# Seven-product pairs in the V chunk and three more in the first attention chunk of a hybrid encoder layer

## The chip, the cores and the metric

One NeuronCore of a Trainium2 chip. The metric is the device time of one execution in microseconds (us), as the median of several runs. Beside the runs stands one profiled execution, from which all durations in this text come.

## The reference

One layer on 256 tokens of width 4096: a first layer norm, one input projection to 13,312 columns, two parallel branches, one output projection, the residual and a last layer norm. All inputs and outputs are float32.

```python
h = layer_norm(x, emb_ln_g, emb_ln_b)
p = h @ w_in                                  # 4096 -> 13312
y_conv = c_b * centred_short_conv(c_c * c_h, conv_w) * jax.nn.silu(c_z)
y_attn = banded_window_attention(a_q, a_k, a_v, sink) * jax.nn.silu(a_z)
y = jnp.concatenate([y_conv, y_attn], axis=-1) @ w_out
out = layer_norm(DN_ALPHA * h + y, ln_g, ln_b)
```

The four kv heads make K and V 512 columns wide each; the sixteen query heads are taken four at a time.

## The kernel before, in words

**Chunks and steps.** The columns of `w_in` are cut into 26 chunks of 512. The first is K, the second V; then come, for each of four head groups, the gate of the attention branch (`C_AZ`) and the queries (`C_Q`); then the convolution's chunks. `w_out` follows in nine chunks. A chunk's sum over the 4096 rows, 32 blocks of 128 ("k-tiles"), is made in steps, which one list (`IN_STEPS`) puts in order. This text numbers the steps from K's first, 0. K has the steps 0 to 7, V 8 to 15, the first attention chunk (the gate of head group 0) 16 to 25, the queries behind it begin with 26.

**Kinds of step.** Everything is multiplied as float32r with a split: a number is kept as a high part and a remainder (low part), and a product takes high by high, high by low and low by high.
- A *plain* step ("s") takes four k-tiles, for two halves of the tokens, two halves of the columns and three products: 48 matmuls of 256 columns (`mm`, line 251). The 32 with the weights' high part come first, then the 16 with the low part.
- A *pair* step ("S") takes two k-tiles as a 2 x 2 matrix of blocks and needs seven block products in place of eight: 7 x 3 = 21 matmuls (`mm_pair`, lines 276 and 277 with the high part, 14 matmuls, then 279 with the low part, 7). It needs sums of blocks of x (made once for each pair of k-tiles, `x_sums`, kept in `SC`) and of blocks of the weights (made for every step, `sums`, lines 183 to 185).
- A *half* step ("h") takes two k-tiles in the plain way: 24 matmuls.

`PAIRS` gives the number of pairs of each chunk and `ORDERS` the order of its steps: 0 pairs, `"ssssssss"`; 4 pairs (`NP1`), `"sssSSsSsSs"`; 7 pairs (`NP`), `"sSShSsSSsSSs"`. A chunk of p pairs takes its first 2p k-tiles by pairs.

**What each engine does in step j** (the loop at line 805): TensorE multiplies step j. ScalarE writes the high part of the weights of step j + 3 (`split_hi`, line 204), then what is due at that step (`later`). VectorE does what is due, then `x_sums` if the step is in `X_SUMS`, then the block sums of step j + 4 if that is a pair, then the low part of step j + 3 (`split_lo`, line 208). SyncE issues the loads of coming pieces as buffers come free. Every engine executes its list in the order in which it is written; there is no scheduler.

**Buffers.** There are three tiles for high parts (`whi`), three for low parts (`wlo0` to `wlo2`), three for loaded pieces (`w0` to `w2`), and a fourth (`w6`) from the end of the prologue on. A chunk's sums stand in two of four PSUM tiles (`acc`). A chunk with pairs uses two more PSUM banks (`pacc`), of which there are only two: the first pair of the next chunk opens them again, after `pair_sums` has read them. Before, the first chunk with pairs is the first attention chunk.

**Chunk ends.** A chunk without pairs is taken from PSUM at the end of its last step (`chunk_end`). For a chunk with pairs `pair_copy` and `pair_sums` (lines 679 to 682) turn the two banks into sums in SBUF right behind its last pair, and four steps behind the chunk's last step `whole` (line 687) adds what stands in `acc`. K is copied out, transposed and split (`k_turn`, one step later); V is split into high and low part straight from PSUM (`end_v`), for two of the heads into `v` and for the others into `vlate`, which goes to DRAM for later.

**x.** The prologue normalises x, turns it (`hT`) and splits it into `xT`, four k-tiles at a time (`x_split(q)`, lines 385 and 386). The first eight k-tiles of K are multiplied straight from `hT`, so that K doesn't need their split. `x_sums(p)` makes the sums of pair p (four on VectorE from `xs`, lines 645 and 650, then high parts on ScalarE and low parts on VectorE, `halves`, lines 497 and 498) and overwrites one block of `xT` with one of them; so it can stand only behind the last plain step that uses these two k-tiles.

Of the kernel before, what the change touches and what calls it, by code (L numbers as in the profile page):

```python
# [34 lines left out]
NPC = KT // PK  # L35
IN_ORDER = [C_K, C_V]
# [5 lines left out]
HT = S // 2  # L42
NP = 7
NP1 = 4
PAIRS = [0, 0, NP1] + [NP] * (len(IN_ORDER) - 3)
ORDERS = {0: "s" * 8, NP1: "sssSSsSsSs", NP: "sSShSsSSsSSs"}
OUT = 100
OP = 4
# [6 lines left out]
def units(ci):  # L55


    q, p, us = -(-2 * PAIRS[ci] // PK), 0, []
    for u in ORDERS[PAIRS[ci]]:
        if u == "s":  # L60
            us.append(("in", ci, q))
            q += 1
        elif u == "h":
            us.append(("half", ci, PAIRS[ci]))
        else:
            us.append(("pair", ci, p))
            p += 1
    assert q == NPC and p == PAIRS[ci]
    return us
# [18 lines left out]
def npairs(ci):  # L88
    return PAIRS[ci] if ci < OUT else OUT_ORDERS[ci - OUT].count("S")

# [10 lines left out]
def encoder_kernel(ctx: ExitStack, tc: tile.TileContext, x, emb_g, emb_b, wi, ws, conv_w, sink, wo, ln_g, ln_b, out):  # L101
# [28 lines left out]
    def w_bufs(j):  # L130

        bs = [(wpool, f"w{k}") for k in range(N_W)] + (extra if j < N_IN else [])
        if j >= N_IN and R is not None:
            late = j > in_R[0][0]
            bs += [(None, name) for last, name in in_R if j <= last and late == (name == "R2")]
        last_user = lambda b: max(u for c, u in user.items() if c == b or b[1] == "R2" and c[0] is None) if (
            b in user or b[1] == "R2") else -1
        return min((last_user(b), k) for k, b in enumerate(bs)), bs

    def load(j, to=None):  # L140
        kind, a, b = steps[j]
        if to is None:
            (_, k), bs = w_bufs(j)
            pool, name = bs[k]
            user[bs[k]] = j
            if pool is None:
                to = raw[j] = {"R0": R[:, 0, D // 2:D], "R1": R[:, 1, D // 2:D], "R2": R[:, :, 3 * D // 4:D]}[name]
            else:
                to = raw[j] = pool.tile([P, PIECE], F32, name=name, bufs=1)
        src = {"in": (wi, IN_PIECES), "out": (wo, OUT_PIECES)}.get(kind, (ws, ALL_PAIRS))  # L150
        src = src[0][src[1].index((a, b))]
        if len(to.shape) == 3:
            if is_pair(j):
                nc.sync.dma_start(out=to[:, 0, :], in_=src)
            else:
                nc.sync.dma_start(out=to, in_=src.rearrange("p (i n) -> p i n", i=2))
        else:
            nc.sync.dma_start(out=to[:, 0:src.shape[1]], in_=src)
# [43 lines left out]
    def split_hi(j):  # L202
        wh[j] = half_tile(j, "whi")
        nc.scalar.activation(part(j, wh[j]), part(j, raw[j]), AF.Copy)  # L204

    def split_lo(j):
        wl[j] = half_tile(j, "wlo")
        nc.vector.tensor_tensor(part(j, wl[j]), part(j, raw[j]), part(j, wh[j]).bitcast(F32), op=ALU.subtract)  # L208
        raw.pop(j)

    def split(j):
        if j < len(steps):
            split_hi(j)
            split_lo(j)
# [14 lines left out]
    for name in ("whi", "w0", "w1", "w2", "wlo0", "m", "nm", "wlo1", "den", "es", "wlo2"):  # L229
        n = {"whi": PIECE + GAP}.get(name, PIECE + 2 * OFF if name[:3] == "wlo" else PIECE if name[0] == "w" else 2)  # L230
# [3 lines left out]
    acc = {}  # L234
# [58 lines left out]
    with tc.tile_pool(name="pro", bufs=1) as pro:  # L293
# [62 lines left out]
        def transp2(q, tiles=(0, 1)):  # L356
            for half in range(2):
                if tiles[0] == 0:
                    pair[q, half] = ps_att.tile([P, 2, S], F32, name="att")
                for k in range(2):  # L360
                    kt = q * 4 + half * 2 + k
                    for i in tiles:
                        nc.tensor.transpose(pair[q, half][:, k, i * P:(i + 1) * P], xs[i][:, kt * P:(kt + 1) * P],  # L363
                                            ident)
# [18 lines left out]
        def x_split(q):  # L383
            sl = slice(q * 4, q * 4 + 4)
            nc.vector.tensor_copy(xT[:, sl, 0:S], hT[:, sl, :])
            nc.vector.tensor_tensor(xT[:, sl, S:2 * S], hT[:, sl, :], xT[:, sl, 0:S].bitcast(F32), op=ALU.subtract)
# [49 lines left out]
        turned2(5)  # L436
        x_split(5)
        split(5)
        load(8)
        transp2(6)  # L440
        mm(4)
        turned2(6)
        x_split(6)
        split(6)
        load(9)
        transp2(7)
        mm(5)
# [4 lines left out]
        mm(6)  # L452
        split(8)
        load(11)
        x_split(0)
        split(9)
        load(12)
        x_split(1)
    n_pro = 7


# [13 lines left out]
    def build_tab():  # L475
        ti = pa.tile([P, 2, S], F32, name="ti", tag="s")
        nc.gpsimd.iota(ti, pattern=[[-P, 2], [1, S]], base=0, channel_multiplier=-1,
                       allow_small_or_imprecise_dtypes=True)
        tf = pa.tile([P, 2, S], F32, name="tf", tag="p", bufs=2)
        nc.vector.tensor_scalar(tf, ti, -1.0, None, op0=ALU.mult)  # L480
        nc.vector.tensor_tensor(tf, tf, ti, op=ALU.max)
        nc.vector.tensor_scalar(ti, tf, float(WINDOW), NEG, op0=ALU.is_gt, op1=ALU.mult)
        nc.vector.tensor_tensor(tab, ti, tf, op=ALU.subtract)
# [12 lines left out]
    def halves(hi, lo, src):  # L496
        nc.scalar.activation(hi, src, AF.Copy)
        nc.vector.tensor_tensor(lo, src, hi.bitcast(F32), op=ALU.subtract)
# [18 lines left out]

    def end_v(ci, g):
        late = pa.tile([P, 2, 2, 2, P], F32R, name="vlate", tag="qhl")
        for i in range(2):  # L520
            ps = acc.pop((ci, i)).rearrange("p (a n) -> p a n", a=4)
            halves(v[:, :, i, 0, :], v[:, :, i, 1, :], ps[:, 0:2, :])
            halves(late[:, :, i, 0, :], late[:, :, i, 1, :], ps[:, 2:4, :])
        nc.sync.dma_start(out=vd, in_=late.bitcast(F32))
# [159 lines left out]
    def whole(ci):  # L684
        t = st_.pop(("e", ci))
        for i in range(2):
            nc.vector.tensor_tensor(t[:, i, :], acc.pop((ci, i)), t[:, i, :], op=ALU.add)
        return t
# [63 lines left out]
        for hi, lo, y in y_parts(q):  # L752
            nc.vector.tensor_tensor(lo, y, hi.bitcast(F32), op=ALU.subtract)

    X_SUMS = [NPC + 2 + k for k in range(NP1)] + [2 * NPC + k for k in (1, 4, 6)]
    build_tab()
    later = {}

    def at(j, fn, *a):
        later.setdefault(j, []).append((fn, a))  # L760

    ENDS = [(C_AZ, end_z), (C_V, end_v), (C_K, end_k), (C_Q, end_q), (C_CZ, end_cz), (C_CH, end_ch), (C_CC, end_cc),
            (C_CB, end_cb)]

# [32 lines left out]
    nxt = n_pro + 6  # L797
    last0 = N_IN - len(ORDERS[PAIRS[-1]])
    for t, f, q in ((3, y_load, 0), (5, y_hi, 0), (6, y_lo, 0), (6, y_load, 1), (7, y_hi, 1), (8, y_lo, 1), (8, y_load, 2),
# [5 lines left out]
    for j in range(n_pro, N_IN):  # L805
        kind, ci, q = steps[j]
# [8 lines left out]
        if kind == "pair" and q == PAIRS[ci] - 1:  # L815
            pair_copy(ci)
            at(j + 1, pair_sums, ci)
        if j in X_SUMS:
            x_sums(X_SUMS.index(j), pa.tile([P, 4 * S], F32, name="xs", tag="zT", bufs=2))
        if steps[j + 1][1] != ci or j == N_IN - 1:  # L820
# [235 lines left out]
    n = ncs - 1  # L1056
# [78 lines left out]
```

## Time and profile before

| | before |
|---|---|
| time, median of 3 runs (lowest to highest) | 1506.08 us (1505.47 to 1506.26) |
| the profiled execution, its time | 1505.99 us |
| the profiled execution, span of its instructions | 1504.3 us |
| TensorE's granted clock, mean | 0.999 |
| bytes moved by DMA | 316.18 MB, 210 GB/s on average |

The span runs from the first to the last instruction of the core; the execution's own time is 1.7 us longer. The profile was read by its list of engines, the chain of work that ended last, the table of who waited for whom, the timeline of each engine (start in us, length in us, engine, line, operation, output from input, count, and in brackets the idle time before it and what ended it) and busy times by stretches of time.

### The profile page before, as it was taken

The numbers are of one execution on the slowest core, as the hardware profiler recorded it, in microseconds if no ns is written. First come the engines' busy times: TensorE is split into PE (matmuls) and PEld (weight loads), VectorE is DVE, ScalarE is ACT, GpSimd is POOL, SyncE is SP. The second block draws the span as 40 slices with busy tenths as digits, with TensorE's granted clock in tenths as the row PEclk, the third lists the DMA queues.
The fourth block names the chain that finished last, engine by engine and source line by source line (L and its number), as shares of the span: only waits on it lengthen the run. The fifth ranks groups of instructions, "written<-read, shape, count | busy, mean of one in ns | idle before, by whom it ended". The sixth has DMA issues, their size and how long they took to land.

```text
span 1504.3 us, 30113 instructions
## 1 busy us (share of the span) xinstructions
PE 1490.8 (99%) x12947; PEld 1475.4 (98%) x12947; DVE 1329.7 (88%) x1555; ACT 781.7 (52%) x669; POOL 1.3 (0%) x7
## 2 busy tenths in 40 slices
PE   7999999999999999999999999999999999999998
PEld 4999999999999999999999999999999999999997
DVE  7768989999899998999899999999899688888876
ACT  4545556656566665545555455544556444444431
POOL 0000000000000000000000000000000000000000
PEclk9999999999999999999999999999999999999999
DMA  7555555656555555656556655656557656766673
GB/s 289 217 182 197 210 197 170 208 183 207 196 186 190 181 186 206 233 197 238 187 195 218 220 197 196 220 184 227 205 206 297 261 204 219 261 217 217 219 261 123
DMA packets 71749, 316.18 MB, mean 210 GB/s; under 512 B 8544, under 2 KB 12608, under 8 KB 50880
## 3 DMA queue, kind: packets, MB, share of 16 engines
q1 hardware_dynamic: 70608, 312.43, 58.7%
q8 instruction: 101, 1.65, 0.4%
q10 hardware_dynamic: 1008, 1.84, 0.3%
q14 instruction: 32, 0.26, 0.1%
HBM read 305.23 MB, written 8.91 MB: 209 GB/s over the span
## 4 chain that ended last, share of the span: by engine, by line
PE 98%; DVE 1%; DMA 0%; ACT 0%; SPq 0%; issue 0%; ACTq 0%
PE acc L251 45%; PE acc L923 20%; PE pacc L276 6%; PE pacc L277 6%; PE pacc L279 6%; PE acc L277 4%; PE acc L276 4%; PE acc L279 4%; PE att L493 1%; PE att L618 1%; DVE st L330 0%; PE att L604 0%; PE acc L380 0%; DMA x<-in_x 0%; PE att L363 0%; DVE x L338 0%
## 5 line engine op out<-in xcount | busy, mean ns | idle before, releaser
L204 ACT ACTIVATE whi<-w 128x2048 fp32r<-128x2048 f32 (+1 forms) x354 | 621.7, 1761 | 593.8 <-DVE w L185 231.0
L208 DVE TENSOR_TENSOR wlo<-w,whi 128x2048 fp32r<-128x2048 f32 (+1 forms) x354 | 736.1, 2083 | 102.7 <-ACT whi L204 83.6
L251 PE MATMUL acc<-whi,xT 128*128 128x256 f32 x3952 | 474.0, 276 | 0.0
L251 PEld LDWEIGHTS acc<-whi,xT 128*128 128x128 f32 x3952 | 459.9, 188 | 0.0
L251 PE MATMUL acc<-wlo,xT 128*128 128x256 f32 x1976 | 245.8, 275 | 0.0
L251 PEld LDWEIGHTS acc<-wlo,xT 128*128 128x128 f32 x1976 | 234.0, 188 | 0.0
L923 PE MATMUL acc<-whi,xT 128*128 128x256 f32 x1696 | 201.8, 275 | 0.0
L923 PEld LDWEIGHTS acc<-whi,xT 128*128 128x128 f32 x1696 | 196.6, 188 | 0.4 <-issue 0.4
L183 DVE TENSOR_TENSOR w<-w 128x512 f32<-128x512 f32 x179 | 122.4, 684 | 8.3 <-DMA w<-in_ws 8.3
L923 PE MATMUL acc<-wlo,xT 128*128 128x256 f32 x848 | 105.3, 275 | 0.0
L276 PE MATMUL acc<-whi,xT 128*128 128x256 f32 x370 | 102.1, 276 | 0.0
L277 PE MATMUL acc<-whi,xT 128*128 128x256 f32 x370 | 102.1, 276 | 0.0
L923 PEld LDWEIGHTS acc<-wlo,xT 128*128 128x128 f32 x848 | 100.4, 188 | 0.0
L276 PE MATMUL pacc<-whi,xT 128*128 128x256 f32 x350 | 98.2, 281 | 0.0
L277 PE MATMUL pacc<-whi,xT 128*128 128x256 f32 x350 | 96.5, 276 | 0.0
L279 PE MATMUL pacc<-wlo,xT 128*128 128x256 f32 x350 | 96.2, 275 | 0.0
L279 PE MATMUL acc<-wlo,xT 128*128 128x256 f32 x370 | 92.8, 275 | 0.0
L277 PE MATMUL pacc<-whi,SC 128*128 128x256 f32 x330 | 91.0, 276 | 0.0
L276 PE MATMUL pacc<-whi,SC 128*128 128x256 f32 x330 | 91.0, 276 | 0.0
L279 PE MATMUL pacc<-wlo,SC 128*128 128x256 f32 x330 | 82.9, 275 | 0.0
L184 DVE TENSOR_TENSOR w<-w 128x256 f32<-128x256 f32 x179 | 76.1, 425 | 6.2
L185 DVE TENSOR_TENSOR w<-w 128x256 f32<-128x256 f32 x179 | 76.1, 425 | 6.2
(220 smaller groups left out, 1674.3 us busy)
## 6 DMA issues: line engine op xcount, KB each, us to landing
w<-in_wi SPq DMA_DIRECT2D x112, 1024.0 KB
w<-in_ws SPq DMA_DIRECT2D x202, 512.0 KB
w<-in_wo SPq DMA_DIRECT2D x41, 1024.0 KB
R<-in_wo SPq DMA_DIRECT2D x13, 1024.0 KB
x<-in_x SPq DMA_DIRECT2D x7, 512.0 KB
yl<-yd SPq DMA_DIRECT2D x7, 512.0 KB
xc<-in_x SPq DMA_DIRECT2D x14, 256.0 KB
R<-in_ws SPq DMA_DIRECT2D x6, 512.0 KB
```

The costliest lines, as they stand in the source:

```text
L183: nc.vector.tensor_tensor(s01, b22, b12.to_broadcast([P, 2, HW]), op=ALU.add)
L184: nc.vector.tensor_tensor(r(6), r(5), r(1), op=ALU.add)
L185: nc.vector.tensor_tensor(r(7), r(6), r(3), op=ALU.add)
L204: nc.scalar.activation(part(j, wh[j]), part(j, raw[j]), AF.Copy)
L208: nc.vector.tensor_tensor(part(j, wl[j]), part(j, raw[j]), part(j, wh[j]).bitcast(F32), op=ALU.subtract)
L251: nc.tensor.matmul(acc[ci, i][:, c:c + HW], x, w[:, k * W + c:k * W + c + HW], start=(first and w is hi and k + off + c == 0), stop=(last ...
L276: nc.tensor.matmul(o, ah, hi[:, w, :], start=(opens and p == 0), stop=False)
L277: nc.tensor.matmul(o, al, hi[:, w, :], start=False, stop=False)
L279: nc.tensor.matmul(o, ah, lo[:, w, :], start=False, stop=(closes and last))
L493: nc.tensor.transpose(ps[:, c, i * P:(i + 1) * P], t[:, i, (2 * b + c) * P:(2 * b + c + 1) * P], ident)
L618: nc.tensor.matmul(o_ps, v[:, g, kb, part_, :], t[:, 0, kb, :], start=(kb + part_ == 0), stop=False)
L923: nc.tensor.matmul(acc[ci, i][:, c:c + HW], y, m[:, k * w + c:k * w + c + HW], start=(first and off + c == 0), stop=(last and c + HW == w))
```

## The change

V gets four pair steps (steps 8 to 17 now, `"sssSSsSsSs"`), and the first attention chunk seven (18 to 29, `"sSShSsSSsSSs"`); all other chunks keep theirs. The splits of x's first eight k-tiles, which pairs 0 to 3 need, are made two and three steps earlier, in K's steps. The seven sums of x, which were made in the steps 10 to 13, 17, 20 and 22, are made in the steps 7, 8, 9, 10, 12, 14 and 16. V's end takes the sum of `acc` and of the pairs' part from SBUF (`whole`), in step 21.

```diff
-PAIRS = [0, 0, NP1] + [NP] * (len(IN_ORDER) - 3)
+PAIRS = [0, NP1] + [NP] * (len(IN_ORDER) - 2)
 ORDERS = {0: "s" * 8, NP1: "sssSSsSsSs", NP: "sSShSsSSsSSs"}
...
         split(5)
+        x_split(0)
         load(8)
...
         split(6)
+        x_split(1)
         load(9)
...
         load(11)
-        x_split(0)
         split(9)
         load(12)
-        x_split(1)
...
     def end_v(ci, g):
         late = pa.tile([P, 2, 2, 2, P], F32R, name="vlate", tag="qhl")
+        t = whole(ci)
         for i in range(2):
-            ps = acc.pop((ci, i)).rearrange("p (a n) -> p a n", a=4)
+            ps = t[:, i, :].rearrange("p (a n) -> p a n", a=4)
             halves(v[:, :, i, 0, :], v[:, :, i, 1, :], ps[:, 0:2, :])
             halves(late[:, :, i, 0, :], late[:, :, i, 1, :], ps[:, 2:4, :])
...
-    X_SUMS = [NPC + 2 + k for k in range(NP1)] + [2 * NPC + k for k in (1, 4, 6)]
+    X_SUMS = [NPC + k for k in (-1, 0, 1, 2, 4, 6, 8)]
```

Three places of VectorE's list show what the numbers of the tables do to it. The first is V up to the end of step 10 (before: from the end of step 8 on). `wlo` is a low part, `xs`, `SC` and `xT` belong to the sums of x, `w` with lines 183 to 185 are the block sums of the weights of a pair; a line behind 516 stands one further in the changed kernel. Before:

```order
L208 TENSOR_TENSOR wlo_795<-w_624,whi 128x2048
L208 TENSOR_TENSOR wlo_849<-w_632,whi 128x2048
L645 TENSOR_TENSOR xs<-xT 128x512
L650 TENSOR_TENSOR xs<-xs 128x128 x4
L498 TENSOR_TENSOR SC<-xs,SC 128x384
L498 TENSOR_TENSOR xT<-xs,xT 128x128
L208 TENSOR_TENSOR wlo_913<-w_721,whi 128x2048
```

and in the change, from the end of the sums of x of pair 2, which now stand in step 9:

```order
L498 TENSOR_TENSOR SC<-xs,SC 128x384
L498 TENSOR_TENSOR xT<-xs,xT 128x128
L208 TENSOR_TENSOR wlo_885<-w_634,whi 128x1792
L646 TENSOR_TENSOR xs<-xT 128x512
L651 TENSOR_TENSOR xs<-xs 128x128 x4
L498 TENSOR_TENSOR SC<-xs,SC 128x384
L498 TENSOR_TENSOR xT<-xs,xT 128x128
L183 TENSOR_TENSOR w_816<-w_816 128x512
L184 TENSOR_TENSOR w_816<-w_816 128x256
L185 TENSOR_TENSOR w_816<-w_816 128x256
L208 TENSOR_TENSOR wlo_952<-w_731,whi 128x2048
```

The low part that step 9 makes (`wlo_849` before, `wlo_885` now) has become that of a pair and has sums of x ahead of it, and in step 10 block sums for a pair four steps ahead stand in front of step 13's low part (`wlo_913` before, `wlo_952` now).

The second place is step 16 to step 17, V's last pair and last step, behind which the first attention chunk begins. In the change:

```order
L498 TENSOR_TENSOR SC_642<-xs,SC_642 128x384
L498 TENSOR_TENSOR xT<-xs,xT 128x128
L183 TENSOR_TENSOR w_1110<-w_1110 128x512
L184 TENSOR_TENSOR w_1110<-w_1110 128x256
L185 TENSOR_TENSOR w_1110<-w_1110 128x256
L208 TENSOR_TENSOR wlo_1211<-w_1073,whi 128x1792
L680 TENSOR_TENSOR q<-q,pacc 128x256
L681 TENSOR_TENSOR q<-pacc,q 128x256
L682 TENSOR_TENSOR q<-q,pacc 128x256
L683 TENSOR_TENSOR q<-pacc,q 128x256
L208 TENSOR_TENSOR wlo_1269<-w_1110,whi 128x1792
```

Lines 680 to 683 are the pair sums of V; before, V had none, and what stood at V's end were its four quarters from PSUM:

```order
L208 TENSOR_TENSOR wlo_1159<-w_975,whi 128x2048
L498 TENSOR_TENSOR v<-acc,v 128x2x128
L498 TENSOR_TENSOR vlate<-acc,vlate 128x2x128
L498 TENSOR_TENSOR v<-acc,v 128x2x128
L498 TENSOR_TENSOR vlate<-acc,vlate 128x2x128
L183 TENSOR_TENSOR w_1103<-w_1103 128x512
```

So the last reader of the two `pacc` banks, which step 19 opens again, now stands behind the seventh set of sums of x, a set of block sums and the low part of step 19.

The third place is step 21, where V now ends, in the middle of the first attention chunk. In the change:

```order
L208 TENSOR_TENSOR wlo_1387<-w_1267,whi 128x2048
L688 TENSOR_TENSOR q<-acc,q 128x512 x2
L498 TENSOR_TENSOR v<-q,v 128x2x128
L498 TENSOR_TENSOR vlate<-q,vlate 128x2x128
L498 TENSOR_TENSOR v<-q,v 128x2x128
L498 TENSOR_TENSOR vlate<-q,vlate 128x2x128
L183 TENSOR_TENSOR w_1355<-w_1355 128x512
L184 TENSOR_TENSOR w_1355<-w_1355 128x256
L185 TENSOR_TENSOR w_1355<-w_1355 128x256
L208 TENSOR_TENSOR wlo_1432<-w_1323,whi 128x1792
```

The four quarters of v have moved from V's end to this place, with the two additions of `whole` ahead of them; the low part behind them (`wlo_1432`) is that of step 24, a pair.

## The prediction

> **What bounds the kernel now.** I read the page first (sections 1 and 4), then who waits for whom on TensorE, then both engines' busy time over the two stretches that the change rewrites: the V chunk (67.24 to 111.69 us) and the first attention chunk behind it (to 152.40).
>
> ```profile
> span 1504.3 us, 30113 instructions
> PE 1490.8 (99%) x12947; PEld 1475.4 (98%) x12947; DVE 1329.7 (88%) x1555; ACT 781.7 (52%) x669; POOL 1.3 (0%) x7
> PE 98%; DVE 1%; DMA 0%; ACT 0%; SPq 0%; issue 0%; ACTq 0%
> ```
> ```profile
> PE att L393 <- DMA x<-in_x: 8.6, 1, 8.6
> PE att L983 <- ACT lhs L965: 0.4, 1, 0.4
> PE acc L345 <- DVE x L338: 0.3, 1, 0.3
> ```
> ```profile
> core 0: us, PE busy (x) PEld busy (x) DVE busy (x) ACT busy (x) POOL busy (x), PEclk, DMA share, GB/s
> 67.24:111.69 44.45, 44.45 (x394) 44.45 (x393) 30.58 (x42) 19.82 (x21) 0.00 (x0) 1.00 0.52 190
> 111.69:152.40 40.71, 40.71 (x362) 40.71 (x361) 35.87 (x52) 20.27 (x21) 0.00 (x0) 1.00 0.51 183
> ```
>
> TensorE is the chain that ends last (98%), and after the start it waits for nobody for more than 0.4 us. So a matmul less is time gained, and any wait that is put into TensorE is time lost in full, since no slack comes later. VectorE has 44.45 - 30.58 = 13.87 us spare in V and 40.71 - 35.87 = 4.84 us behind it. That spare is the budget of this change.
>
> **What it removes.** TensorE's rate, and the ends of two kinds of step:
>
> ```profile
> 84.49 3.79 PE L251 MATMUL acc<-whi,xT 128*128 128x256 f32 x32
> ...
> 122.57 3.79 PE L251 MATMUL acc<-whi,xT 128*128 128x256 f32 x32
> 126.20 1.98 PE L251 MATMUL acc<-wlo,xT 128*128 128x256 f32 x16
> 128.01 0.28 PE L276 MATMUL pacc<-whi,xT 128*128 128x256 f32 x1
> ```
> ```profile
> 132.77 3.45 PE L251 MATMUL acc<-whi,xT 128*128 128x256 f32 x29
> ```
>
> A plain step (48 matmuls) takes 128.01 - 122.57 = 5.44 us, its low part beginning 3.63 us in; two pair steps (42) take 132.77 - 128.01 = 4.76, 2.38 each. All are 0.1133 us a matmul. V turns two plain steps (96) into four pairs (84), the attention chunk two plain steps (96) into three pairs and a half step (63 + 24 = 87). That is 21 matmuls less, **-2.38 us**, the whole gain.
>
> **What it adds: VectorE's list.** Its prices are distances from one start to the next, in rows without foreign waits:
>
> ```profile
> 46.21 0.69 DVE L385 CAST xT<-hT 128x1024 fp32r<-128x1024 f32 x1 [2.22 <-ACT hT L371]
> ...
> 52.59 0.69 DVE L385 CAST xT<-hT 128x1024 fp32r<-128x1024 f32 x1 [2.22 <-ACT hT L371]
> ...
> 64.36 0.68 DVE L385 CAST xT<-hT 128x1024 fp32r<-128x1024 f32 x1
> 65.07 1.22 DVE L386 TENSOR_TENSOR xT<-hT,xT 128x1024 fp32r<-128x1024 f32 x1
> 67.11 0.43 DVE L480 TENSOR_SCALAR tf<-ti 128x512 f32<-128x512 f32 x1 [0.81 <-POOL ti L477]
> ...
> 69.36 2.28 DVE L208 TENSOR_TENSOR wlo<-w,whi 128x2048 fp32r<-128x2048 f32 x1
> 73.95 0.69 DVE L498 TENSOR_TENSOR kT<-att,kT 128x512 fp32r<-128x512 f32 x1 [2.30 <-ACT kT L497]
> ...
> 75.15 2.28 DVE L208 TENSOR_TENSOR wlo<-w,whi 128x2048 fp32r<-128x2048 f32 x1
> ```
> ```profile
> 114.43 0.42 DVE L498 TENSOR_TENSOR vlate<-acc,vlate 128x256 fp32r<-128x256 f32 x1 [0.45 <-ACT vlate L497]
> 114.77 0.68 DVE L183 TENSOR_TENSOR w<-w 128x512 f32<-128x512 f32 x1
> ...
> 116.29 2.28 DVE L208 TENSOR_TENSOR wlo<-w,whi 128x2048 fp32r<-128x2048 f32 x1
> 118.50 0.68 DVE L183 TENSOR_TENSOR w<-w 128x512 f32<-128x512 f32 x1
> ...
> 120.01 2.02 DVE L208 TENSOR_TENSOR wlo<-w,whi 128x1792 fp32r<-128x1792 f32 x1
> 121.95 0.69 DVE L645 TENSOR_TENSOR xs<-xT 128x512 f32<-128x512 f32 x1
> ...
> 124.28 0.56 DVE L498 TENSOR_TENSOR SC<-xs,SC 128x384 fp32r<-128x384 f32 x1 [0.59 <-ACT SC L497]
> ...
> 124.96 2.02 DVE L208 TENSOR_TENSOR wlo<-w,whi 128x1792 fp32r<-128x1792 f32 x1
> ```
> ```profile
> 154.60 0.41 DVE L679 TENSOR_TENSOR z<-z,pacc 128x256 f32<-128x256 f32 x1
> ...
> 156.30 2.02 DVE L208 TENSOR_TENSOR wlo<-w,whi 128x1792 fp32r<-128x1792 f32 x1
> ...
> 159.76 1.22 DVE L208 TENSOR_TENSOR wlo<-w,whi 128x1024 fp32r<-128x1024 f32 x1
> ...
> 168.53 1.28 DVE L687 TENSOR_TENSOR z<-acc,z 128x512 f32<-128x512 f32 x2
> 169.73 0.68 DVE L183 TENSOR_TENSOR w<-w 128x512 f32<-128x512 f32 x1
> ```
> ```profile
> 129.85 1.71 ACT L204 ACTIVATE whi<-w 128x1792 fp32r<-128x1792 f32 x1 [1.48 <-PE pacc L277]
> ```
>
> Sums of x: 121.95 to 124.96, 3.01 us (0.59 of it the trip through ScalarE). Block sums of a pair: 1.51. Low split: 1.94 for a pair, 2.21 for a plain piece, 1.14 for a half one (1.22 less the 0.08 by which neighbours overlap: 2.28 against 2.20). Pair sums at a chunk's end: 1.70; `whole`: 1.20; a quarter of v: 0.34; kT and klate: 1.20. A split's result counts 0.10 us behind its successor's start (0.08 of overlap, the rest for the hand-over, an estimate).
>
> The two moved **splits of x** take 1.85 us each (64.36 to 65.07 + 1.22, less overlap) and fall into the two idle stretches of 2.22 us before 46.21 and 52.59: cost nothing; without that cover 1.85 each would be late for K's next low split. In return the table of distances follows the split of step 9 at once (64.36), so VectorE runs: table 2.25 to 66.61, sums of x for pair 0 to 69.62, block sums for step 11 to 71.13, split 10 to 73.34. That is ahead of kT, which starts at 73.95 as before, because TensorE's transposes set it. From there VectorE's list is closed up. I write the time at which each entry is done and the next can start, steps in parentheses:
>
> kT, klate 75.15; sums of x 78.16; block sums (12) 79.67; split (11) 81.61; sums of x 84.62; split (12) 86.56; sums of x 89.57; block sums (14) 91.08; split (13) 93.29; split (14) 95.23; sums of x 98.24; block sums (16) 99.75; split (15) 101.96; split (16) 103.90; sums of x 106.91; split (17) 109.12; block sums (19) 110.63; split (18) 112.84; sums of x 115.85; block sums (20) 117.36; split (19) 119.30; V's pair sums 121.00; split (20) 122.94; block sums (22) 124.45; half split (21) 125.59; split (22) waits for ScalarE's high split, which starts behind the block sums and takes 1.71, to 126.30, then 128.24; block sums (24) 129.75; split (23) 131.96; `whole` 133.16; four quarters of v 134.52; block sums (25) 136.03; split (24) 137.97.
>
> TensorE without waits would start step 11 at 84.49 (where step 10 ended before), 12 at 86.87, 13 at 89.25, 14 at 94.69, 15 at 97.07, 16 at 102.51, 17 at 104.89, 18 at 110.33, 19 at 115.77, 20 at 118.15, 21 at 120.53, 22 at 123.25, 23 at 125.63, 24 at 131.07. A plain step needs its low split 3.63 us in, a pair 14 x 0.1133 = 1.59 in. The lateness that VectorE forces, counted from this timetable:
> - step 13: 93.39 against 92.88, 0.51 us;
> - step 15: 102.06 against 100.70, 1.36;
> - step 19 opens the two PSUM banks that V's pair sums still read. The first is free after the first of the four sums (119.30 + 0.41 and 0.05), 119.76 against 115.77: 3.99. The second, opened 8 matmuls later, is free at 121.13 against 116.68: 4.45;
> - step 24, behind `whole` and v: 138.07 against 132.66, **5.41**.
>
> Steps 11, 12, 14, 16, 17, 18, 20 to 23 are in time once these waits are in. Lateness isn't added up but carried: new waits of 0.51, 0.85, 2.63, 0.46 and 0.96. Behind step 24 split (25) is done at 139.91 against 140.5, and the chunks from there on have the list that they have now, without waits. Behind a waiting matmul stand all others of TensorE, and ScalarE's splits wait for it too (their buffers), but they are needed three steps later.
>
> Moved at no cost: the sums' two ScalarE copies each (ScalarE is busy 19.82 of 44.45 us); v's copies and store, now in step 21, read a chunk later; four more DMA issues for the same bytes (pieces of half size). Transfers were late for block sums four times in 179, 8.3 us together, in
>
> ```profile
> L183 DVE TENSOR_TENSOR w<-w 128x512 f32<-128x512 f32 x179 | 122.4, 684 | 8.3 <-DMA w<-in_ws 8.3
> ```
>
> so 0 to 3 us here; I take 0, as most of the 179, because a piece's buffer is asked for some steps ahead.
>
> **The sum.** -2.38 + 5.41 = +3.03 us on the profiled execution's 1505.99 us (span 1504.3 and 1.7 around it): 1509.0. The median of the runs shown, 1506.08, lies 0.09 above it, which gives **1509.1 us**. Unknown is the sum's last per cent: a 1% error of VectorE's 64 us from 73.95 on is 0.64 us, so 1508.5 to 1509.8.
>
> **The rivals.** *The clock falls* (20%). TensorE stands still for 2.63 us, works 0.9 and stands for 0.46. It has no such hole now, except at the end:
>
> ```profile
> 1494.50:1497.90 3.40, 3.04 (x12) 1.15 (x10) 3.33 (x8) 0.87 (x2) 0.00 (x0) 1.00 0.23 80
> 1497.90:1501.30 3.40, 2.33 (x6) 0.66 (x5) 1.52 (x3) 1.19 (x2) 0.00 (x0) 1.00 1.01 379
> 1501.30:1504.30 3.00, 0.00 (x0) 0.00 (x0) 0.00 (x0) 0.00 (x0) 0.00 (x0) 0.50 0.48 180
> ```
>
> There the granted clock goes to 0.50 right behind 3.4 us in which TensorE was busy for 2.33; with 3.04 it stayed at 1.00. Were it lowered behind step 19's wait for as long as that wait took (3.1 us), half of it is lost, 1.55, of which step 24's 0.96 comes back (that time is VectorE's): +0.6, 1509.7; for twice as long 3.1 - 0.96 = +2.1, 1511.2. The Trainium skill, "TensorE: Matmul & The Clock Gate", Part 1, says that about 3.4 us of idleness halves the clock and an equal busy window restores it: by its figure 1.7 us would be lost and, by estimate, 1509.8 result, against 1509.1 by the holes of this trace that change nothing. This trace agrees on the half clock, but it came after a window that was not idle.
>
> *The last wait is covered* (13%). If v's quarters or step 22's 0.7 us of waiting come cheaper, step 19's 4.45 decides: +2.07, 1508.1.
>
> *VectorE's list is short enough* (3%, the side of faster). The mechanism is the trip through ScalarE: 0.59 in each sum of x, six of them from 75.15 on, 3.5 us. The change pays from the point where the lateness at step 24 falls under 2.38, so the list must shrink by 3.0. If all six trips vanished, at step 24 1.9 would remain and the time be 1505.6; without any wait it is 1503.7. Against it: the same 0.59 would have to go although VectorE executes in order and the next entry needs the copy.
>
> *A transfer is late* (2%): up to 3 us on a wait, 1511 to 1512. That the products are not saved at all is excluded by the order of matmuls, which shows the pairs.
>
> **How the numbers follow.** The forecast (62%) straddles the bound of 0.2%, 3.0 us, about what a measurement of this kernel can tell from no change: I give 33 to above and 29 to below it. Slower: 33 + 20 + 2 = 55%; within 0.2%: 29 + 13 = 42%; faster 3%. The range reaches from the covered wait, 1508.1 less a margin of 0.2, to 1510.9, over the clock's smaller price; left out are its long form, the late transfer and the faster case, about 10%.
>
> **What would show it.** In the profile after: TensorE has 21 matmuls less; its waits name VectorE's `wlo` in the low parts of L251 (two, some 0.5 and 0.9 us) and of L279 (one, 1.0), and a pair's first L276 that waits 2.6 us for pair sums into `q`; VectorE has no idle gap over 0.8 us from 75 to 135 us; later chunks look as before, 3 us later. Wrong would be: no wait at the first pair of the attention chunk, a granted clock under 1.00 near 122 us, new waits behind 140 us, or idle VectorE in V.

## The result, and the profile after

| | before | after |
|---|---|---|
| median of 11 runs | 1506.00 us (1505.33 to 1506.35) | 1509.49 us (1508.81 to 1509.74) |
| ratio after/before | | 1.0024, 95% interval 1.0016 to 1.0031 |
| profiled execution | 1505.99 us, span 1504.3 | 1509.62 us, span 1507.9 |

The kernel became 3.5 us slower, where 3.0 had been forecast. The head of the page of the changed kernel (busy time and instructions of each engine, and the shares of the chain that ended last):

```profile
span 1507.9 us, 30129 instructions
PE 1491.6 (99%) x12926; PEld 1475.4 (98%) x12926; DVE 1347.7 (89%) x1586; ACT 787.0 (52%) x674; POOL 1.3 (0%) x7
PE 96%; DVE 3%; DMA 0%; ACT 0%; issue 0%; SPq 0%; DVEq 0%; ACTq 0%
```

TensorE (PE) executes 12947 - 12926 = 21 matmuls less, so the saving was made. But VectorE's share of the chain has risen from 1% to 3%. What TensorE waits for in the changed kernel (who, for whom, us in total, times, longest):

```profile
PE att L393 <- DMA x<-in_x: 8.7, 1, 8.7
PE pacc L276 <- DVE q L680: 2.4, 1, 2.4
PE acc L251 <- DVE wlo L208: 0.9, 2, 0.5
PE att L984 <- ACT lhs L966: 0.4, 1, 0.4
```

Three new waits on VectorE. The wait of step 24 on `wlo` (L279) that had been forecast is not among them. Where they stand shows TensorE's timeline of the changed kernel (start, us, group, idle time before it and who ended it):

```profile
89.42 3.79 PE L251 MATMUL acc<-whi,xT 128*128 128x256 f32 x32
93.59 2.13 PE L251 MATMUL acc<-wlo,xT 128*128 128x256 f32 x16 [0.39 <-DVE wlo L208]
...
97.94 3.79 PE L251 MATMUL acc<-whi,xT 128*128 128x256 f32 x32
102.26 2.12 PE L251 MATMUL acc<-wlo,xT 128*128 128x256 f32 x16 [0.53 <-DVE wlo L208]
...
115.66 1.98 PE L251 MATMUL acc<-wlo,xT 128*128 128x256 f32 x16
120.02 0.35 PE L276 MATMUL pacc<-whi,xT 128*128 128x256 f32 x1 [2.38 <-DVE q L680]
...
121.49 0.41 PE L276 MATMUL pacc<-whi,SC 128*128 128x256 f32 x1
...
123.98 0.28 PE L279 MATMUL pacc<-wlo,SC 128*128 128x256 f32 x1
124.10 0.28 PE L276 MATMUL pacc<-whi,xT 128*128 128x256 f32 x1
...
138.64 0.28 PE L279 MATMUL pacc<-wlo,xT 128*128 128x256 f32 x1
```

From start to start, the low part of step 13 comes 93.59 - 89.42 - 3.63 = 0.54 us late, that of step 15 102.26 - 97.94 - 3.63 = 0.69, and step 19 starts at 120.02, where step 18 leaves off at 115.66 + 16 x 0.1133 = 117.47: 2.55. (The bracket says less each time, since the matmul ahead is still in flight when the wait begins.) Then comes something else: step 19, a pair, takes from 120.02 to 124.10, 4.08 us in place of 2.38, with no wait in it. Both engines' busy time, the granted clock (PEclk) and the DMA share in stretches around it, in the changed kernel:

```profile
117.07:120.47 3.40, 1.01 (x10) 0.85 (x9) 3.30 (x6) 2.65 (x2) 0.00 (x0) 1.00 0.00 0
120.47:123.88 3.41, 3.41 (x19) 3.41 (x18) 3.34 (x5) 0.00 (x0) 0.00 (x0) 0.50 0.87 312
123.88:124.60 0.72, 0.72 (x8) 0.72 (x8) 0.69 (x2) 0.00 (x0) 0.00 (x0) 1.00 0.67 102
```

For 3.41 us behind a window in which TensorE was busy for 1.01 of 3.40, the granted clock is 0.50; this text calls that the half clock. Step 19's matmuls start 0.213 us apart in it, against 0.1133 before, and with some 0.1 us for the slow start of its first matmul that makes the 1.70 us (4.08 - 2.38) that the step takes longer. VectorE's side in the changed kernel, at kT and at the end of the list:

```profile
74.11 0.69 DVE L498 TENSOR_TENSOR kT<-att,kT 128x512 fp32r<-128x512 f32 x1 [0.53 <-ACT kT L497]
...
77.65 0.56 DVE L498 TENSOR_TENSOR SC<-xs,SC 128x384 fp32r<-128x384 f32 x1 [0.59 <-ACT SC L497]
...
119.47 0.41 DVE L680 TENSOR_TENSOR q<-q,pacc 128x256 f32<-128x256 f32 x1
...
120.82 0.42 DVE L683 TENSOR_TENSOR q<-pacc,q 128x256 f32<-128x256 f32 x1
...
136.34 2.02 DVE L208 TENSOR_TENSOR wlo<-w,whi 128x1792 fp32r<-128x1792 f32 x1
```

From kT to the split of step 24 the list took 136.34 - 74.11 = 62.23 us. The low part of step 24 could have begun at 136.34 + 1.94 + 0.10 = 138.38 and began at 138.64, because the clock had held TensorE back by more than VectorE's list asked.

The account: against the timetable of the prediction the low part of step 24 is 138.64 - 132.66 = 5.98 us late: 0.17 from a start that was later in this execution (step 13 begins at 89.42, not 89.25), 0.54, 0.69 and 2.55 of waits, 2 x 0.15 because the two low parts that waited got going slowly (2.13 and 2.12 us against 1.98), and 1.70 in step 19, nearly all of it the half clock, 5.95 in all. Less 2.38 for the matmuls, 5.98 gives 3.60, and the spans differ by 3.6.

### The profile page after: what moved, and what is told of

The parts are those of the page before. It is cut to its first block, busy times and chain, and to the rows that moved or that the text cites. A ratio compares the mean times of both kernels' runs of the same rounds, so it can differ in the third digit from the quotient of the medians.

```text
span 1507.9 us, 30129 instructions
## 1 busy us (share of the span) xinstructions
PE 1491.6 (99%) x12926; PEld 1475.4 (98%) x12926; DVE 1347.7 (89%) x1586; ACT 787.0 (52%) x674; POOL 1.3 (0%) x7
## 4 chain that ended last, share of the span: by engine, by line
PE 96%; DVE 3%; DMA 0%; ACT 0%; issue 0%; SPq 0%; DVEq 0%; ACTq 0%
PE acc L251 41%; PE acc L924 20%; PE pacc L276 6%; PE pacc L277 6%; PE pacc L279 6%; PE acc L277 4%; PE acc L276 4%; PE acc L279 4%; DVE wlo L208 1%; PE att L493 1%; PE acc L380 1%; PE att L619 1%; PE att L605 0%; DMA x<-in_x 0%; DVE xs L651 0%; PE att L363 0%
## 5 line engine op out<-in xcount | busy, mean ns | idle before, releaser
L251 PE MATMUL acc<-whi,xT 128*128 128x256 f32 x3840 | 460.8, 276 | 0.0
L251 PEld LDWEIGHTS acc<-whi,xT 128*128 128x128 f32 x3840 | 446.9, 188 | 0.0
L251 PE MATMUL acc<-wlo,xT 128*128 128x256 f32 x1920 | 239.3, 275 | 0.9 <-DVE wlo L208 0.9
L251 PEld LDWEIGHTS acc<-wlo,xT 128*128 128x128 f32 x1920 | 227.5, 188 | 1.3 <-DVE wlo L208 1.3
L924 PEld LDWEIGHTS acc<-whi,xT 128*128 128x128 f32 x1696 | 196.6, 188 | 0.4 <-issue 0.4
L183 DVE TENSOR_TENSOR w<-w 128x512 f32<-128x512 f32 x186 | 127.1, 683 | 7.8 <-DMA w<-in_ws 7.8
L276 PE MATMUL pacc<-whi,xT 128*128 128x256 f32 x364 | 102.3, 281 | 2.4 <-DVE q L680 2.4
L277 PE MATMUL pacc<-whi,xT 128*128 128x256 f32 x364 | 100.5, 276 | 0.0
L924 PEld LDWEIGHTS acc<-wlo,xT 128*128 128x128 f32 x848 | 100.4, 188 | 0.0
L279 PE MATMUL pacc<-wlo,xT 128*128 128x256 f32 x364 | 100.3, 275 | 0.0
L279 PE MATMUL acc<-wlo,xT 128*128 128x256 f32 x384 | 96.6, 276 | 0.0
L277 PE MATMUL pacc<-whi,SC 128*128 128x256 f32 x344 | 95.1, 277 | 0.0
L276 PE MATMUL pacc<-whi,SC 128*128 128x256 f32 x344 | 95.1, 277 | 0.0
L279 PE MATMUL pacc<-wlo,SC 128*128 128x256 f32 x344 | 86.6, 276 | 0.0
L184 DVE TENSOR_TENSOR w<-w 128x256 f32<-128x256 f32 x186 | 79.1, 425 | 6.5
L185 DVE TENSOR_TENSOR w<-w 128x256 f32<-128x256 f32 x186 | 79.1, 425 | 6.4
```

The costliest lines, as they stand in the source:

```text
L183: nc.vector.tensor_tensor(s01, b22, b12.to_broadcast([P, 2, HW]), op=ALU.add)
L184: nc.vector.tensor_tensor(r(6), r(5), r(1), op=ALU.add)
L185: nc.vector.tensor_tensor(r(7), r(6), r(3), op=ALU.add)
L251: nc.tensor.matmul(acc[ci, i][:, c:c + HW], x, w[:, k * W + c:k * W + c + HW], start=(first and w is hi and k + off + c == 0), stop=(last ...
L276: nc.tensor.matmul(o, ah, hi[:, w, :], start=(opens and p == 0), stop=False)
L277: nc.tensor.matmul(o, al, hi[:, w, :], start=False, stop=False)
```

## The experiments

Each kernel is the changed one with the edit shown, unless the text says otherwise; times are medians, and before stood at about 1505.9 us in all of them. Three questions were open: whether VectorE's list does it, what the half clock costs, and which of the list's entries decides.

**1. Is it VectorE's list? The splits of x back where they were**

```diff
-        x_split(0)
-        x_split(1)
...
+        x_split(0)
+        x_split(1)
```

> The change with the first two splits of x at their old places, behind the low splits of the steps 8 and 9. Theory 1 (from kT on VectorE's list is closed up, so what is put in ahead of step 11 comes out at its end one for one): the second split (1.85 us) and the table that waits for it come 2.2 us later and push kT's successors by 2.2 us; step 11 waits 0.4, step 13 2.3 us; time 1511.6, ratio 1.0037. Theory 2 (VectorE has idle time in between that takes it up): as the change, 1509.5, ratio 1.0024.

Measured: 1511.74 us (1510.88 to 1511.97, 5 runs), ratio 1.0038 (1.0025 to 1.0051): 2.25 us over the changed kernel. TensorE's waits on VectorE in this kernel:

```profile
PE acc L251 <- DVE wlo L208: 2.6, 2, 2.0
PE pacc L276 <- DVE q L680: 2.4, 1, 2.4
...
PE pacc L279 <- DVE wlo L208: 0.3, 1, 0.3
```

What VectorE loses ahead of kT appears as a longer wait for the first low parts (2.0 us at step 13), so the list is closed up from there, and time on it is time of the kernel, one for one: 2.2 us were expected, 2.25 measured. So moving the splits spares the change 2.25 us.

**2. Pairs in one chunk alone.** First the pairs in V, with the first attention chunk as before:

```diff
-PAIRS = [0, NP1] + [NP] * (len(IN_ORDER) - 2)
+PAIRS = [0, NP1, NP1] + [NP] * (len(IN_ORDER) - 3)
```

> The change with four pairs in the first attention chunk as before (the sums of x as in the change): 12 matmuls less, -1.36 us. Theory 1 (lateness is carried along one list): the waits at step 13 (0.6) and step 15 (0.8) stay, nothing later, since V's end and the attention chunk have room now: +1.43 - 1.36 = +0.1, ratio 1.0000, no change. Theory 2 (each pair costs VectorE's share by itself, so the loss divides as the pairs do, 4 of 7 of 3.5 us): +2.0, ratio 1.0013.

Measured: 1505.94 us (1505.67 to 1506.64, 11 runs), ratio 1.0001 (0.9992 to 1.0010). Only the two waits in L251 remain (0.9 us). Then seven pairs in the attention chunk alone, V and its end as before (`end_v` is put back too, which this cut of the edit leaves out):

```diff
-PAIRS = [0, NP1] + [NP] * (len(IN_ORDER) - 2)
+PAIRS = [0, 0] + [NP] * (len(IN_ORDER) - 2)
...
-    X_SUMS = [NPC + k for k in (-1, 0, 1, 2, 4, 6, 8)]
+    X_SUMS = [NPC + 2 + k for k in range(NP1)] + [2 * NPC + k for k in (1, 4, 6)]
```

> No pairs in V (its end as before), seven in the first attention chunk, the sums of x as before the change: 9 matmuls less, -1.02 us. Theory 1: VectorE is late once, 2.3 us at a pair near 145 us, since two sets of sums of x stand in this chunk: +1.3, ratio 1.0009; the clock may fall behind a wait of that length, and then 1.7 us more are lost, as no later wait is there to be replaced: up to +3.0. Theory 2 (shares by pairs, 3 of 7): +1.5.

Measured: 1507.76 us (1507.54 to 1509.79, 11 runs), ratio 1.0016 (1.0007 to 1.0025). Seven runs lie at 1507.54 to 1507.81, four at 1509.20 to 1509.79 (experiment 5 asks why). The lower group is 1.7 us over before, where 1.3 was expected. By the span of its instructions it is 1.3 (1505.6 in the profiled execution against 1504.3); the rest lies outside the span, 2.0 to 2.1 us here in place of 1.7, for a cause that stays open. The profile has one wait for it:

```profile
146.49 0.39 PE L279 MATMUL pacc<-wlo,xT 128*128 128x256 f32 x1 [2.06 <-DVE wlo L208]
```

Either half alone costs less (0 and 1.9 by the medians) than both together (3.5). Neither is free of lateness, but each has some of VectorE's spare to itself.

**3. Later sums of x**, four sets where they were, three put off to steps further on:

```diff
-    X_SUMS = [NPC + k for k in (-1, 0, 1, 2, 4, 6, 8)]
+    X_SUMS = [NPC + k for k in (-1, 0, 1, 2, 12, 15, 17)]
```

> The change with the sums of x for pairs 4, 5 and 6 in the steps 20, 23 and 25 instead of 12, 14 and 16. Theory 1 (what counts is the length of the list from V to the next chunk's begin, which has little room until then): the wait at step 19 goes, and lateness appears behind it, 1.4 us at step 24 and 3 to 4.5 us more by step 31: +4.1, ratio 1.0027, the clock holds, because no wait is over 1.9 us. Theory 2 (the sums were only made too early, ahead of work that is due sooner): at least the 3.4 us of step 19 come back, 1506 or less.

Measured: 1510.50 us (1510.30 to 1510.68, 6 runs), ratio 1.0030 (1.0019 to 1.0042). The waits go to other places and grow, in this kernel:

```profile
PE pacc L279 <- DVE wlo L208: 2.1, 2, 1.3
PE acc L251 <- DVE wlo L208: 2.0, 2, 1.6
PE acc L276 <- ACT SC L497: 0.6, 1, 0.6
```

The longest wait is 1.6 us, and the clock of this profile stays at 1.00 up to the kernel's end. Putting whole sets of sums off doesn't make the list shorter, so the lateness only moves.

**4. What the half clock costs.** Ten multiplications of the unit matrix (each recorded as two), into a bank that nobody reads, keep TensorE busy in the hole ahead of step 19:

```diff
+        if (ci, kind, q) == (2, "pair", 0):
+            fill = ps_att.tile([P, W], F32, name="att")
+            for _ in range(10):
+                nc.tensor.matmul(fill[:, 0:P], ident, ident, start=True, stop=True)
         mm_pair(j) if kind == "pair" else mm(j)
```

> Ten multiplications of the 128 x 128 unit matrix by itself (20 records of 0.112 us, 2.2 us) stand on TensorE ahead of step 19, in the 2.5 us in which it waits for V's pair sums; they write a PSUM bank that nobody reads. Theory 1 (VectorE's list alone sets the time; the half clock cost little, since the wait at step 24 would have come in its place): the clock stays at 1.00, step 19 takes 2.4 us and a short wait instead of 4.1, a wait of about 1.0 us at step 24 appears, and the time is only 0.3 to 0.4 us below the change's: 1509.1, ratio 1.0021. Theory 2 (the half clock of 3.4 us is a loss on top): 1.7 us below the change's, 1507.8, ratio 1.0012.

Measured: 1509.12 us (1509.04 to 1509.50, 11 runs), ratio 1.0022 (1.0013 to 1.0031). TensorE's timeline and one stretch of the kernel with the filler:

```profile
116.97 2.39 PE L815 MATMUL att<-ident 128*128 128x128 f32 x20
119.52 0.36 PE L276 MATMUL pacc<-whi,xT 128*128 128x256 f32 x1 [0.15 <-DVE q L680]
```
```profile
120.00:124.00 4.00, 3.88 (x33) 3.68 (x33) 3.90 (x6) 0.00 (x0) 0.00 (x0) 1.00 0.77 279
```

The clock stays at 1.00. And the two waits that were missing come back, on the second bank of step 19 and at step 24, in the same kernel:

```profile
120.40 0.28 PE L277 MATMUL acc<-whi,xT 128*128 128x256 f32 x1
120.80 0.38 PE L276 MATMUL pacc<-whi,SC 128*128 128x256 f32 x1
...
136.82 0.28 PE L277 MATMUL pacc<-whi,SC 128*128 128x256 f32 x1
137.90 0.39 PE L279 MATMUL pacc<-wlo,xT 128*128 128x256 f32 x1 [0.81 <-DVE wlo L208]
```

From start to start, less one matmul of 0.1133, they are 0.29 and 0.97 us. So the 1.70 us of step 19 are no loss of 1.70: most of them stand where TensorE would have waited for VectorE anyway. The medians differ by 0.37 (0.27, when each is taken against the kernel before as measured beside it), and the two ratios' intervals overlap: that the half clock costs so little is shown by theory 2's 1507.8 not coming, its exact price is not. The changed kernel's own eleven runs fit: eight took 1509.47 to 1509.74 us, with mean clocks of 0.998 (seven) and 0.999, and three took 1508.81 to 1509.21, with 0.999 and 1.000 (two).

**5. The two groups of the attention chunk alone.** Experiment 2's second kernel, with eight such multiplications ahead of the matmul that waits there:

```diff
+        if (ci, p) == (2, 5):
+            fill = ps_att.tile([P, W], F32, name="att")
+            for _ in range(8):
+                nc.tensor.matmul(fill[:, 0:P], ident, ident, start=True, stop=True)
```

> The kernel with pairs in the attention chunk only, with eight multiplications of the unit matrix (1.8 us) on TensorE ahead of the low part of step 25, where it stood for 2.06 us. That kernel's eleven runs fell into two groups, seven from 1507.54 to 1507.81 and four from 1509.2 to 1509.79. Theory 1 (in some runs the hole falls into one window of the clock's controller and halves the clock for 3.4 us, a loss of 1.7 us): with the hole filled all runs lie near 1507.6, none above 1508.5. Theory 2 (the two groups come from something else, a transfer or the start): about a third of the runs stays near 1509.4.

Measured: 1507.66 us (1507.43 to 1508.10, 11 runs), ratio 1.0012 (1.0003 to 1.0021). The upper group is gone. That a wait of 2.06 us halves the clock in some executions and not in others fits this, but no profile caught one of the four. (Their mean clocks were 0.998 and 0.999, those of the lower group 0.999 and 1.000.)

What the profiles do show is why the same hole can go either way. In all twelve, the moments at which the granted clock is recorded to change are whole multiples of 3.4133 us apart. In the changed kernel it falls at 120.47 us, rises at 123.88 and falls again at 1506.28, near the kernel's end: 1 and 405 times 3.4133. So in these profiles the clock changes only at the bounds of windows of that length. In the changed kernel's profile the hole (117.47 to 120.02) lies whole in the window before 120.47. In the profile of experiment 2's second kernel, one of the lower group, the clock first falls at 1503.78 us; counted back from there, a bound at 145.27 cuts the hole (144.26 to 146.49) in two:

```profile
141.86:145.27 3.41, 2.56 (x23) 2.37 (x21) 2.99 (x6) 1.12 (x3) 0.00 (x0) 1.00 0.63 267
145.27:148.69 3.42, 2.20 (x19) 2.21 (x20) 3.42 (x3) 3.42 (x3) 0.00 (x0) 1.00 0.35 85
```

Behind either window the clock stays at 1.00. That the four slower executions had the hole in one window is likely by this, and not shown.

**6. The trip through ScalarE.** Each set of sums of x makes VectorE wait for ScalarE's copies (0.59 us in the row above). Here the copies are issued at the same place, and VectorE takes up the two low parts later, behind the block sums or the low split:

```diff
-        halves(SC[p][:, 0, :, :], SC[p][:, 1, :, :], s[:, 0:3, :])
-        halves(x[:, 0, HT:2 * HT], x[:, 0, 3 * HT:4 * HT], s[:, 3, :])
+        pieces = ((SC[p][:, 0, :, :], SC[p][:, 1, :, :], s[:, 0:3, :]),
+                  (x[:, 0, HT:2 * HT], x[:, 0, 3 * HT:4 * HT], s[:, 3, :]))
+        for hi, _, src in pieces:
+            nc.scalar.activation(hi, src, AF.Copy)
+        for hi, lo, src in pieces:
+            lows.append((lo, src, hi))
...
+    def x_lows():
+        for lo, src, hi in lows:
+            nc.vector.tensor_tensor(lo, src, hi.bitcast(F32), op=ALU.subtract)
+        lows.clear()
...
         sums(j + 4)
+        if j + 4 < len(steps) and is_pair(j + 4):
+            x_lows()
...
+        x_lows()
```

> The change, with the two low parts of each set of sums of x put behind the block sums (or, in steps without block sums, behind the low split) instead of straight behind the sums, so that VectorE doesn't wait for ScalarE's high parts (0.59 us each time). The same instructions, another order. Theory 1: the list from kT on is some 4 us shorter, lateness at step 24 falls from 5.4 to 1.4 us (0.5 at step 19, 1.0 at step 24), the clock holds, and the time is 1505.1, ratio 0.9994, 0.95 us below before. Theory 2 (the list is not what decides, but the place of V's pair sums ahead of step 19): the wait at step 19 stays over 2 us, 1509, ratio 1.002.

Measured: 1504.95 us (1504.79 to 1505.16, 11 runs), ratio 0.9994 (0.9985 to 1.0003). VectorE's timeline in this kernel, beside the change's 74.11 and 77.65:

```profile
73.77 0.69 DVE L498 TENSOR_TENSOR kT<-att,kT 128x512 fp32r<-128x512 f32 x1 [1.21 <-ACT kT L497]
...
75.69 1.02 DVE L651 TENSOR_TENSOR xs<-xs 128x128 f32<-128x128 f32 x4
76.63 0.69 DVE L183 TENSOR_TENSOR w<-w 128x512 f32<-128x512 f32 x1
...
78.15 0.55 DVE L767 TENSOR_TENSOR SC<-xs,SC 128x384 fp32r<-128x384 f32 x1
...
131.91 2.02 DVE L208 TENSOR_TENSOR wlo<-w,whi 128x1792 fp32r<-128x1792 f32 x1
```

The block sums (L183) begin right behind the sums (75.69 + 1.02), and the low part finds its copy ready: no idle time is shown. From kT to the split of step 24 the list takes 131.91 - 73.77 = 58.14 us, 4.09 less than in the change; some 4 were expected. The same instructions in another order are worth 1509.49 - 1504.95 = 4.54 us. Of the change's three waits none is left in the table of waits, and step 24's takes their place in this kernel:

```profile
PE pacc L279 <- DVE wlo L208: 0.8, 1, 0.8
```

**7. The same order in the kernel before**, so that the order isn't credited with more than it does. To `x_sums` and `x_lows`, as in experiment 6, come the same two calls:

```diff
+        if j + 4 < len(steps) and is_pair(j + 4):
+            x_lows()
...
+        x_lows()
```

> The kernel before (four pairs in the first attention chunk, none in V), with the low parts of the sums of x put behind the block sums as in the faster versions. Theory 1: TensorE waits for nobody there, so a shorter list of VectorE gives nothing: 1505.9, ratio 1.0000, and the gain of the faster versions is that of the 21 matmuls. Theory 2 (the order is worth something by itself): 1505 or less, ratio under 0.9995.

Measured: 1505.90 us (1505.66 to 1506.59, 11 runs), ratio 1.0000 (0.9991 to 1.0009). Where VectorE has slack, the trips cost nothing and their removal brings nothing.

**8. One set of sums ahead of kT.** The kernel of experiment 6, with the second, third and fourth set each a step earlier, so that two instead of one stand ahead of kT, where VectorE waits (1.21 us in the fence of experiment 6), and the split of step 9 behind the table of distances:

```diff
-        split(9)
-        load(12)
...
-    X_SUMS = [NPC + k for k in (-1, 0, 1, 2, 4, 6, 8)]
+    X_SUMS = {7: (0, 1), 8: (2,), 9: (3,), 12: (4,), 14: (5,), 16: (6,)}
     build_tab()
+    split(9)
+    load(12)
...
-        if j in X_SUMS:
-            x_sums(X_SUMS.index(j), pa.tile([P, 4 * S], F32, name="xs", tag="zT", bufs=2))
+        for p in X_SUMS.get(j, ()):
+            x_sums(p, pa.tile([P, 4 * S], F32, name="xs", tag="zT", bufs=2))
```

> As the kernel with the low parts behind, and the table of distances ahead of the low split of step 9, in the 3.1 us in which VectorE waits for ScalarE there, with the sums of x for pair 1 in step 7 as well (those for pairs 2 and 3 in steps 8 and 9). Theory 1: the list behind kT is shorter by one more set of sums, 2.4 us, no wait is left, and all 21 matmuls come out: 1503.6, ratio 0.9984. Theory 2 (a wait that the list hid, kT's or a transfer's, comes instead): 1505 or above, ratio 0.9994 or above.

Measured: **1503.33 us** (1503.09 to 1503.58, 11 runs), ratio 0.9983 (0.9974 to 0.9992), the only one here that is faster than before by more than its interval. The two stretches of the page's first reading, in this kernel (columns as above):

```profile
67.24:111.69 44.45, 44.45 (x394) 44.45 (x394) 42.56 (x72) 24.70 (x30) 0.00 (x0) 1.00 0.48 168
111.69:150.00 38.31, 38.31 (x341) 38.31 (x340) 36.98 (x42) 21.15 (x17) 0.00 (x0) 1.00 0.65 221
```

TensorE is busy without a gap again, VectorE for 42.56 of 44.45 us in V (30.58 before), and the gain, 1505.9 - 1503.33 = 2.57 us, is the 2.38 of the 21 matmuls and about what two medians vary. How the gain over experiment 6 divides between the set ahead of kT and the table ahead of the split of step 9 was not tested.

**9. The sums of x on GpSimd**, additions and low parts, with ScalarE's copies and the order as in the change:

```diff
-        nc.vector.tensor_tensor(lo, src, hi.bitcast(F32), op=ALU.subtract)
+        (eng or nc.vector).tensor_tensor(lo, src, hi.bitcast(F32), op=ALU.subtract)
...
+        add = (eng or nc.vector).tensor_tensor
...
-            x_sums(X_SUMS.index(j), pa.tile([P, 4 * S], F32, name="xs", tag="zT", bufs=2))
+            x_sums(X_SUMS.index(j), pa.tile([P, 4 * S], F32, name="xs", tag="zT", bufs=2), nc.gpsimd)
```

> The change with all additions and low parts of the sums of x on GpSimd (its instructions, 9 a set, are the same; ScalarE's high parts stay), which is idle else (1.3 us busy in all). Theory 1, if GpSimd works beside VectorE: VectorE's list loses 7 times 3 us, no wait is left, 1503.6, ratio 0.9984. Rival: both engines hinder each other, so that what GpSimd does is taken from VectorE after all: 1509.5 if each of GpSimd's instructions costs VectorE what its own cost, more if they are slower. The Trainium skill's page on SBUF says that GpSimd's instructions and those of VectorE with two SBUF operands lock one pair of ports against each other, and its page on GpSimd that additions take about twice as long there: by these, some 1 us a set more than now, about 1515.

Measured: 1509.94 us (1509.78 to 1510.31, 7 runs), ratio 1.0027 (1.0017 to 1.0038). VectorE has less to do in V in this kernel (32.62 us busy, 39.61 in the change over the same stretch), and TensorE waits all the same:

```profile
67.24:111.69 44.45, 43.44 (x380) 43.02 (x378) 32.62 (x24) 19.04 (x25) 39.96 (x36) 1.00 0.46 161
```

GpSimd's sums are slow, and VectorE's instructions beside them slower than otherwise. From the groups of GpSimd between 60 and 130 us, from VectorE's timeline (2.28 and 0.68 for the first two lines elsewhere) and from GpSimd's timeline of this kernel, whose lengths are rough for this engine:

```profile
L652 POOL TENSOR_TENSOR xs<-xs 128x128 f32<-128x128 f32 x28 | 25.8, 941 | 1.1
L647 POOL TENSOR_TENSOR xs<-xT 128x512 f32<-128x512 f32 x6 | 10.0, 1670 | 0.0
```
```profile
67.86 3.12 DVE L208 TENSOR_TENSOR wlo<-w,whi 128x2048 fp32r<-128x2048 f32 x1
...
82.52 0.95 DVE L183 TENSOR_TENSOR w<-w 128x512 f32<-128x512 f32 x1
...
87.00 2.89 DVE L208 TENSOR_TENSOR wlo<-w,whi 128x2048 fp32r<-128x2048 f32 x1 [2.32 <-ACT whi L204]
```
```profile
68.78 2.52 POOL L498 TENSOR_TENSOR xT<-xs,xT 128x128 fp32r<-128x128 f32 x1
...
86.02 0.46 POOL L498 TENSOR_TENSOR xT<-xs,xT 128x128 fp32r<-128x128 f32 x1
```

Much of GpSimd's slowness comes from VectorE: the same subtraction takes it 2.52 us while VectorE's low split runs (67.86 to 70.98) and 0.46 while VectorE stands idle (the 2.32 us before 87.00). Of the two prices of the rival the lower one (1509.5) came near, the 1515 did not.

And ScalarE, which executes in order, has its copy of a sum ahead of the next high split, in the same kernel:

```profile
84.43 0.52 ACT L497 ACTIVATE SC<-xs 128x384 fp32r<-128x384 f32 x1 [5.21 <-POOL xs L652]
85.06 1.91 ACT L204 ACTIVATE whi<-w 128x2048 fp32r<-128x2048 f32 x1
```

It stands still for 5.21 us for GpSimd, and the high split, VectorE's low split and TensorE stand behind it. How much of the time is due to this and how much to the slower VectorE was not told apart.

## Why the prediction was right, and where it was not

- **The saving, -2.38 us:** right. 21 matmuls are gone, and where nothing waits (experiment 8) 2.57 us are gained.
- **VectorE's list decides:** right, and its prices too: 62.08 us from kT to the split of step 24 were forecast (73.95 to 136.03), 62.23 measured. Experiments 1, 6 and 8 move it each way, and the time follows.
- **Waits of 0.51, 0.85 and 2.63 us:** measured 0.54, 0.69 and 2.55.
- **0.46 at the second bank and 0.96 at step 24, the clock at 1.00:** this is the step that failed, and a granted clock under 1.00 near 122 us had been named as a sign of being wrong. Neither wait was there. In their place the clock stood at half for 3.41 us behind the first bank's wait, and step 19 took 1.70 us longer: 1.70 - 0.46 - 0.96 = +0.28. That the time came out so near (1509.49 against 1509.1) is in part luck: what came in place of the two waits happened to be about as long. That was the rival with 20%; its price (+0.6) took the loss as 1.55 and let only step 24's 0.96 come back, though the slower step hid the second bank's wait as well. Experiment 4 shows the forecast as it was meant: with the clock kept up, the two waits are there with 0.29 and 0.97 us, and the time is 1509.12 against 1509.1.
- **Why the chance of that rival was too low:** the trace of before had shown the half clock behind a window with 2.33 of 3.40 us busy, and the forecast itself put TensorE at rest for 2.63 of a like window. By that row it should have been the likelier case, though busy time alone doesn't decide: behind the window with 2.20 us busy of experiment 5 (19 matmuls, against 6 in that row) the clock stayed up. The Trainium skill, "TensorE: Matmul & The Clock Gate", Part 1, has the clock fall after an idle window of some 3.4 us and come back after an equal busy one, the windows running free of the program. The trace agrees on the length (3.41 us) and with free windows (experiment 5: the bounds stand 3.4133 us apart and elsewhere in each profile). It differs on the condition: the window here was not idle, TensorE worked 1.01 us in it.
- **Moved splits at no cost:** right. Put back, they cost 2.25 us.
- **No new waits behind 140 us, the transfers in time:** right, the table of waits names none. Lateness is carried, not added up.
- **The faster side (3%):** the mechanism named there, the trip of 0.59 us in each set of sums, was the right one. The reason against it was wrong: "the next entry needs the copy" is true of the two low parts only, and the block sums or the split behind them can go first. Six trips were priced at 1505.6, experiment 6 measured 1504.95.

## What to carry to other kernels

Work taken from the engine that bounds the kernel is a gain only if the engine that prepares its operands can take on what is added: write that engine's list with its start-to-start prices and compare it with the other's timetable, entry by entry. When the list is too long by a little, look in it first for round trips through a third engine and put independent entries between the two halves: that turned +3.5 us into -0.95 here, and with one set of entries moved ahead of the point from which the list is closed up, and the table of distances into idle time, all of the gain came out. A hole in TensorE's work is priced twice, as a wait and as a clock that may fall behind it, though the second price is partly hidden when the next wait is the same engine's.

## What the runs showed of the hardware

- A hole of 2.55 us was enough to halve TensorE's clock for 3.41 us in the profiled execution of the changed kernel, and by times and mean clocks probably in eight executions of eleven. In the kernel with pairs in the attention chunk alone, where the wait's row has 2.06 (2.38 in the changed kernel), four executions of eleven took 1.7 us more, and filling the hole removed them.
- The granted clock changed only at moments that are whole multiples of 3.4133 us apart, in all twelve profiles. A hole of 2.55 us that lay in one such window was followed by the half clock, one of 2.23 us that a bound cut in two was not. How much work in a window keeps the clock up was not found: it fell behind windows with 1.01 us busy (10 matmuls) and, at the kernel's end, 2.33 (6 matmuls), and not behind one with 1.90 (16 matmuls, 109.93 to 113.34 us in experiment 9).
- A filler of 2.4 us ahead of the waiting matmul keeps the clock up and costs nothing that was not being waited for.
- Beside VectorE, GpSimd's additions took 0.94 us on average for 128x128 and 1.67 for 128x512, where VectorE takes 1.02 for four of the first and 0.68 for one of the second; a subtraction of 128x128 took GpSimd 0.46 with VectorE idle and 2.52 beside its low split. VectorE's own instructions with two inputs in SBUF went from 2.28 to 3.12 and from 0.68 to 0.95 us beside them. The Trainium skill, "SBUF — State Buffer", section on who interferes with whom, says that such VectorE instructions contend with GpSimd's reads through a shared port; these rows agree that they do. The page speaks of one that blocks the other fully: GpSimd's 2.52 us, which ended 0.3 us behind VectorE's instruction, look like that, while VectorE's instructions were slowed by a factor of 1.4.
